# Where the low halves of 32 input-projection weight tiles are made: VectorE's subtraction, or ScalarE and an accumulating transfer

## The chip, the core and the metric

One Trainium2 chip, one of its cores. The metric is device time in microseconds (us) of one execution, the median of several runs. All times are in us unless marked ns. PE is the matrix engine (TensorE), DVE is VectorE, ACT is ScalarE, POOL is GpSimd, SP is SyncE, which only issues transfers here.

## What is computed

One layer of an encoder over 512 tokens of width 1024, all in float32. The part that matters is the first of its three stages, the token mixer, which begins with one wide projection:

```python
def token_mixer(xn, w_in, b_in, ...):
    proj = xn @ w_in + b_in
    (h_q, h_f_fwd, h_f_bwd, h_i, h_g,
     m_q, m_k, m_v, m_o,
     m_ig_fwd, m_ig_bwd, m_fg_fwd, m_fg_bwd) = split_cols(proj, IN_SPLITS)
...
    x = x + token_mixer(rmsnorm(x, ...), w_in[l], ...)
    x = x + cross_attention(rmsnorm(x, ...), rmsnorm(mem, ...), w_q, w_kv, w_o)
    x = x + squared_relu_mlp(rmsnorm(x, ...), w_up[l], w_down[l])
    return rmsnorm(x, norm_final)
```

Four HGRN2 heads and four mLSTM heads are scanned in both directions from `proj`; their outputs, normalised and gated, go through `w_out`. Cross-attention and a squared-ReLU MLP follow.

## The kernel before

**Three products for one.** A float32 product is made of three PE products on the faster type `float32r`. Each operand is split in a high half, which is its value rounded to `float32r`, and a low half, which is the value minus the high half. `mm3` (lines 226 to 229) issues high times high, high times low, low times high. Where the weights are the stationary operand (kind "d"), the low half of the weights, `wl`, is first read by the third product, line 229; where they are the moving operand (kind "t"), by the second, line 228.

**Weight blocks.** All weights lie in DRAM as blocks of 128 x 1024 numbers (512 KB), in the order in which they are used, `SEQ`. Block 4 is the gate projection; blocks 0 to 3 and 5 to 36 are the input projection `w_in`; then come the cross-attention's keys and values, and so on. One block is 24 matmuls of 512 columns. `load(i)` has SP fetch block i into a staging tile `st` (3 buffers). `split(i)` makes the halves in `wh` and `wl` (3 buffers each): ACT copies `st` to `wh`, rounding it, and DVE subtracts:

```python
def split_out(dst_hi, dst_lo, src):
    sc.activation(dst_hi, src, AF.Copy)
    v.tensor_tensor(out=dst_lo, in0=src, in1=dst_hi.bitcast(F32), op=ALU.subtract)
```

In the trace the first is line 223 (`wh<-st` on ACT), the second line 224 (`wl<-st,wh` on DVE).

**How far ahead.** `weights(key)` splits blocks i, i+1 and i+2 and loads block i+3 before the matmuls of block i. As there are three buffers, the halves of block i+2 can be written when PE has finished block i-1. So each split begins when a block begins on PE and is used two blocks later.

**What else goes on.** Between the matmuls of the projection, `tick()` advances at most two chains of the heads' scans. Each is a generator: some matmuls, then DVE and ACT work for its next step. `gates_chain` transposes on PE (lines 527 and 556) around a scan on DVE (lines 545 and 547). `head_out` takes squares on ACT (line 443), a power on POOL (line 169), a product on DVE (line 445) and a transpose on PE (line 452). The memory tokens are normalised in the same way: squares on ACT (line 712), a power on POOL, a scaling on DVE (line 716), transposes on PE (line 725). Each engine has one queue that runs in order; a scheduler that works from an own model of the engines sets these orders when the kernel is built.

**POOL's transfers.** `add_block` (line 891) is used by the MLP: POOL issues a transfer of a weight block that is added into a tile in SBUF (`accum_op=ALU.add`); the destination is of type float32. The first transfer of such a sum does not add.

Of the kernel before, what the change touches and what calls it, by code (L numbers as in the profile page):

```python
# [13 lines left out]
AF = mybir.ActivationFunctionType  # L14
ALU = mybir.AluOpType
# [30 lines left out]
def _split_order():  # L46
    def d(m, c0, n):
        return [("d", m, 0, c0 + P * i) for i in range(n)]

    def t(m, k0, c0, n=4):  # L50
        return [("t", m, k0 + 2 * i, c0) for i in range(n)]

    seq = t("in", 0, 1536) + [("d", "gate", 0, 0)]
    for g in (0, 512, 1024, 2048):
        seq += d("in", g, 2)
    for g in (0, 512, 1024):
        seq += d("in", g + 256, 2)
    seq += d("in", 2560, 2) + d("in", 3072, 2) + d("in", 2304, 2)
    seq += t("in", 0, 3584) + d("in", 4096, 2) + d("in", 4352, 2)
    seq += d("in", 2816, 2) + d("in", 3328, 2)  # L60
    seq += d("kv", 0, 8) + t("kv", 0, 1024) + t("kv", 0, 1536)
    seq += t("out", 0, 0) + t("out", 0, 512)
    seq += d("xq", 0, 8)
    seq += t("xo", 0, 0) + t("xo", 0, 512)
    for f in range(4):
        for j in range(4):
            seq += d("up", 1024 * f + P * j, 1) + d("up", 1024 * f + P * (j + 4), 1)
        seq += [("t", "down", 8 * f + 2 * g + k, 0) for g in range(2) for k in (0, 4)]
        seq += [("t", "down", 8 * f + 2 * g + 4, 512) for g in range(2)]
    seq += [("t", "down", 8 * f + 2 * g, 512) for f in range(4) for g in range(2)]  # L70
    return seq


SEQ = _split_order()
# [5 lines left out]
def trunk(ctx: ExitStack, tc: tile.TileContext, x, mem, wpk, vec, cst, lmask, rmask, rows, out):  # L80
# [5 lines left out]
    v, sc, gp, pe = nc.vector, nc.scalar, nc.gpsimd, nc.tensor  # L86
# [6 lines left out]
    def T(tag, w, bufs, dt=F32):  # L93
        return (sb if w == 516 else big).tile([P, w], dt, tag=tag, name=nm(tag), bufs=bufs)
# [103 lines left out]
    def load(i):  # L198
        if i >= NSTREAM or i in st_tiles:
            return  # L200
        t = T("st", 1024, 3)
        nc.sync.dma_start(out=t, in_=wpk[i])
        st_tiles[i] = t

    def split(i):
        if i >= NSTREAM or i in hl_tiles:
            return
        load(i)
        s = st_tiles[i]
        hi, lo = T("wh", 1024, 3, F32R), T("wl", 1024, 3, F32R)  # L210
        split_out(hi, lo, s)
        hl_tiles[i] = (hi, lo)

    def weights(key):
        i = SIDX[key]
        with (tc.high_priority() if i > 2 else ExitStack()):
            for n in range(i, i + 3):
                split(n)
            load(i + 3)
        return hl_tiles[i]  # L220
# [4 lines that stand above are left out]
# [64 lines left out]
    for t in range(4):  # L289
        xt = xtile[t]  # L290
        ss = tiny(1)
        sc.activation(junk, xt, AF.Square, accum_out=ss)
        r, _ = rstd_of(ss, 1, D)
        with tc.high_priority():
            for g in range(2):
                xg = xt[:, g * 512:g * 512 + 512]
                v.scalar_tensor_tensor(out=xg, in0=xg, scalar=r, in1=gmix[g], op0=ALU.mult, op1=ALU.mult)
                ps = smb()
                for k in range(4):
                    pe.transpose(ps[:, k * P:k * P + P], xg[:, k * P:k * P + P], ident)  # L300
                p3 = ps[:, :].rearrange("p (k t) -> p k t", t=P)
                split_out(ap(xT[g], t * P, [1024, 4], [1, P]), ap(xT[g], 512 + t * P, [1024, 4], [1, P]), p3)
        if t < 2:
            split(t)
# [417 lines left out]
    for k in range(8):  # L722
# [4 lines left out]
        hi, lo = ms[k]  # L727
# [168 lines left out]
    def job(f, n):  # L896

        if n >= len(JOBS):
            if f < 3:
                split(SIDX["d", "up", 0, 1024 * (f + 1)] + n - len(JOBS))  # L900
            return None
        p, g = JOBS[n]
        if p in PLAIN:
            i = block(f, g, *PLAIN[p])
            split(i)
            return hl_tiles[i]
        if (f, n) not in jobs_hl:
            s_ = sums[f, SUMS[p], g]
            hi, lo = T("wh", 1024, 3, F32R), T("wl", 1024, 3, F32R)
            split_out(hi, lo, s_)  # L910
            jobs_hl[f, n] = (hi, lo)
            if p == "P6":
                add_block(s_, block(f, g, 1, 0))
        return jobs_hl[f, n]
# [208 lines left out]
```

## Time and profile before

| | |
|---|---|
| median of 3 runs | 877.57 (877.56 to 878.74) |
| the profiled execution, its own time | 877.47 |
| its span, first to last instruction | 875.7 |
| outside the span | 1.8 |
| PE busy | 853.6 (97%) |
| DVE busy | 576.2 (66%) |
| ACT busy | 415.5 (47%) |
| POOL busy | 67.4 (8%) |
| transfers issued by SP: share of 16 DMA engines | 26.1% |
| transfers issued by POOL: share of 16 DMA engines | 17.2% |
| loads of staging tiles, issue to landing, median | 3.3 |

The profile is of one execution. Busy time of an engine counts its instructions; matmuls are pipelined, so that a matmul of 0.39 starts every 0.23. A wait is put down to the instruction whose semaphore came last. The time of a transfer runs from its issue to its landing, when the last byte is there and whoever waits is told.

### The profile page before, as it was taken

What the parts mean: (1) busy time and instruction counts of PE and PEld (TensorE: products, weight loads), DVE (VectorE), ACT (ScalarE), POOL (GpSimd) and SP (SyncE); (2) the same over time, 40 slices, a digit from 0 to 9 for tenths busy, and PEclk for the clock granted to TensorE, in tenths of its full rate; (3) what the DMA queues carried; (4) which work ended last, traced back from release to release, by engine and by line L of the source; (5) the groups of instructions that cost most, each with busy time, mean ns of one, the idle gap of its engine ahead of it and who ended that gap; (6) DMA issues with size and microseconds to landing.
All of it is one profiled execution on the core that took longest, in us unless ns stands there. A gap on an engine that the chain in (4) does not pass through costs nothing.

```text
span 875.7 us, 11191 instructions
## 1 busy us (share of the span) xinstructions
PE 853.6 (97%) x4198; PEld 709.3 (81%) x4198; DVE 576.2 (66%) x1006; ACT 415.5 (47%) x758; POOL 67.4 (8%) x114
## 2 busy tenths in 40 slices
PE   7999999999999999999999999999999999999995
PEld 5887888888887886888888887888888888888884
DVE  5557688779536987654655445776667656766675
ACT  5235343353358658534544355553355345435544
POOL 2000000010001000000000200002200310121001
PEclk9999999999999999999999999999999999999998
DMA  7322222311234223352212772238945993598322
GB/s 261 135 98 79 73 73 73 117 63 50 73 99 117 97 98 120 121 169 84 85 51 71 194 190 82 92 116 212 284 143 127 238 279 109 150 284 217 115 55 96
DMA packets 32680, 113.58 MB, mean 130 GB/s; under 512 B 3761, under 2 KB 3889, under 8 KB 32626
## 3 DMA queue, kind: packets, MB, share of 16 engines
q1 hardware_dynamic: 23120, 78.84, 26.1%
q0 software_dynamic: 9216, 33.56, 17.2%
q8 instruction: 33, 0.54, 0.2%
q10 hardware_dynamic: 290, 0.47, 0.1%
q14 instruction: 21, 0.17, 0.1%
HBM read 110.76 MB, written 2.10 MB: 129 GB/s over the span
## 4 chain that ended last, share of the span: by engine, by line
PE 49%; DVE 1%; ACT 0%; POOL 0%; issue 0%; POOLq 0%; ACTq 0%
PE mm L228 10%; PE mm L229 10%; PE mm L227 10%; PE sm L997 5%; PE sm L999 5%; PE sm L998 5%; PE mm L999 1%; PE mm L998 1%; PE mm L997 1%; PE sm L229 1%; PE sm L228 1%; PE sm L227 1%; PE sm L770 0%; PE sm L827 0%; DVE vv L922 0%; ACT t L756 0%
## 5 line engine op out<-in xcount | busy, mean ns | idle before, releaser
L223 ACT ACTIVATE wh<-st 128x1024 fp32r<-128x1024 f32 x133 | 140.9, 1059 | 233.1 <-PE mm L228 115.4
L224 DVE TENSOR_TENSOR wl<-st,wh 128x1024 fp32r<-128x1024 f32 x133 | 162.7, 1223 | 124.3 <-ACT wh L223 120.6
L227 PE MATMUL mm<-xT,wh 128*128 128x512 f32 x552 | 219.7, 399 | 0.0
L228 PE MATMUL mm<-xT,wh 128*128 128x512 f32 x552 | 216.4, 392 | 0.2 <-DVE xT L776 0.2
L229 PE MATMUL mm<-xT,wl 128*128 128x512 f32 x552 | 215.8, 391 | 0.0
L228 PEld LDWEIGHTS mm<-xT,wh 128*128 128x128 f32 x552 | 103.8, 188 | 22.7 <-DVE xT L776 2.0
L229 PEld LDWEIGHTS mm<-xT,wl 128*128 128x128 f32 x552 | 103.6, 188 | 21.7 <-issue 0.2
L227 PEld LDWEIGHTS mm<-xT,wh 128*128 128x128 f32 x552 | 103.8, 188 | 21.4 <-issue 1.2
L891 POOL DMA_DIRECT2D as<-in_wpk x48 | 36.6, 772 | 312.1 <-DVE wl L224 188.1
L955 DVE SCALAR_TENSOR_TENSOR t<-mm,rg 128x512 f32<-128x512 f32 x32 | 22.1, 691 | 55.2 <-PE mm L229 55.0
L229 PE MATMUL mm<-wh,yT 128*128 128x512 f32 x128 | 50.6, 395 | 0.0
L227 PE MATMUL mm<-wh,yT 128*128 128x512 f32 x128 | 50.5, 394 | 0.0
L228 PE MATMUL mm<-wl,yT 128*128 128x512 f32 x128 | 50.0, 391 | 0.0
L999 PE MATMUL sm<-wh,yT 128*128 128x512 f32 x128 | 49.8, 389 | 0.0
L998 PE MATMUL sm<-wl,yT 128*128 128x512 f32 x128 | 49.8, 389 | 0.0
L997 PE MATMUL sm<-wh,yT 128*128 128x512 f32 x128 | 49.8, 389 | 0.0
L223 ACT ACTIVATE wh<-as 128x1024 fp32r<-128x1024 f32 x24 | 25.5, 1062 | 33.3 <-PE sm L999 23.7
L224 DVE TENSOR_TENSOR wl<-as,wh 128x1024 fp32r<-128x1024 f32 x24 | 29.4, 1225 | 13.9 <-ACT wh L223 13.9
L378 PEld LDWEIGHTS sm<-a,t 128*128 128x128 f32 x224 | 30.1, 191 | 2.2 <-ACT t L368 0.4
L930 DVE TENSOR_TENSOR vv<-vv,sm 128x512 f32<-128x512 f32 x48 | 31.0, 680 | 1.2 <-PE sm L999 1.2
L368 ACT ACTIVATE t<-a 128x512 f32<-128x512 f32 x28 | 18.4, 674 | 26.3 <-DVE a L431 23.8
L378 PE MATMUL sm<-a,t 128*128 128x128 f32 x224 | 30.9, 285 | 0.0
(258 smaller groups left out, 1513.5 us busy)
## 6 DMA issues: line engine op xcount, KB each, us to landing
st<-in_wpk SPq DMA_DIRECT2D x133, 512.0 KB, 3.3
as<-in_wpk POOLq DMA_DIRECT2D x48, 512.0 KB, 6.7
gate<-in_wpk POOLq DMA_DIRECT2D x16, 512.0 KB, 7.2
as<-in_x SPq DMA_DIRECT2D x4, 512.0 KB, 6.5
vv<-in_x SPq DMA_DIRECT2D x8, 256.0 KB, 4.3
out<-vv SPq DMA_DIRECT2D x7, 256.0 KB, 2.3
a<-in_mem SPq DMA_DIRECT2D x2, 512.0 KB, 3.9
t<-in_rows SPq DMA_DIRECT2D x2, 256.0 KB, 5.9
```

The lines of the kernel that those rows point to most:

```text
L223: sc.activation(dst_hi, src, AF.Copy)
L224: v.tensor_tensor(out=dst_lo, in0=src, in1=dst_hi.bitcast(F32), op=ALU.subtract)
L227: pe.matmul(ps, lhsT=ah, rhs=bh, start=first, stop=False)
L228: pe.matmul(ps, lhsT=ah, rhs=bl, start=False, stop=False)
L229: pe.matmul(ps, lhsT=al, rhs=bh, start=False, stop=last)
L378: pe.matmul(ps[:, z], lhsT=kc[:, z], rhs=ap(q2, w * P, [2 * L, P // (2 * L)], [512 + L, 2], [1, L]), start=True, stop=True)
L891: gp.dma_start(out=dst, in_=wpk[idx], **kw)
L930: v.tensor_tensor(out=z, in0=z, in1=ps, op=ALU.add if sign > 0 else ALU.subtract)
L955: v.scalar_tensor_tensor(out=y, in0=ps, scalar=0.0, in1=rrow[:, 0:512], op0=ALU.max, op1=ALU.mult)
L997: pe.matmul(ps, lhsT=ah, rhs=bh, start=new, stop=False, **fl)
L998: pe.matmul(ps, lhsT=ah, rhs=bl, start=False, stop=False, **fl)
L999: pe.matmul(ps, lhsT=al, rhs=bh, start=False, stop=end and k == 1, **fl)
```

## The change

For blocks 5 to 36, DVE's subtraction is gone. ACT writes minus the rounded weights into `wl`, POOL issues a transfer that adds the block from DRAM to it, and ACT writes `wh` as before. The low half is then the weights minus their high half, as before.

```diff
         hi, lo = T("wh", 1024, 3, F32R), T("wl", 1024, 3, F32R)
-        split_out(hi, lo, s)
+        if SEQ[i][1] == "in" and i > 4:
+
+            sc.activation(lo, s, AF.Copy, scale=-1.0)
+            gp.dma_start(out=lo, in_=wpk[i], accum_op=ALU.add)
+            sc.activation(hi, s, AF.Copy)
+        else:
+            split_out(hi, lo, s)
         hl_tiles[i] = (hi, lo)
```

Six lines are added, so line numbers of the changed kernel from there on are larger by 6 (229 for 223, 533 for 527); the new ones are 213 (minus), 214 (the transfer) and 215 (`wh`).

On ACT, the split of block 10 (`wh_548` before, `wh_553` now), with the sigmoids of a forget gate and the copy out of the gates' transposes behind it. Before:

```order
L223 ACTIVATE wh_548<-st_484 128x1024
L343 ACTIVATE a_90_531<-mm_486,vc 128x512
L345 ACTIVATE a_91_532<-mm_486,misc 128x512
L529 ACTIVATE a_64_372<-sm_541 64x512
L223 ACTIVATE wh_603<-st_552 128x1024
```

and now:

```order
L215 ACTIVATE wh_553<-st_489 128x1024
L213 ACTIVATE wl_554<-st_489 128x1024
L349 ACTIVATE a_90_536<-mm_491,vc 128x512
L351 ACTIVATE a_91_537<-mm_491,misc 128x512
L535 ACTIVATE a_64_374<-sm_546 64x512
L215 ACTIVATE wh_609<-st_558 128x1024
L213 ACTIVATE wl_610<-st_558 128x1024
```

One copy more stands ahead of the sigmoids. Blocks 7 to 27 and 32 to 36 are split in this order; the other six have `wl` ahead of `wh`.

On PE, in block 8 (`wh_445` before, `wh_448` now), the gates' transposes (line 527 before, 533 now). Before:

```order
L227 MATMUL mm_554<-xT_86,wh_445 128x512
L228 MATMUL mm_554<-xT_86,wh_445 128x512
L527 MATMUL sm_541<-cs,a_92_537 128x128 x4
L229 MATMUL mm_554<-xT_86,wl_446 128x512
L227 MATMUL mm_554<-xT_86,wh_445 128x512
L228 MATMUL mm_554<-xT_86,wh_445 128x512
L229 MATMUL mm_554<-xT_86,wl_446 128x512
```

and now:

```order
L235 MATMUL mm_560<-xT_86,wl_449 128x512
L233 MATMUL mm_560<-xT_86,wh_448 128x512
L234 MATMUL mm_560<-xT_86,wh_448 128x512
L235 MATMUL mm_560<-xT_86,wl_449 128x512
L233 MATMUL mm_560<-xT_86,wh_448 128x512
L533 MATMUL sm_546<-cs,a_92_542 128x128 x4
L234 MATMUL mm_560<-xT_86,wh_448 128x512
```

They stand five matmuls later, and so do the transposes of line 556 that follow in the next block.

On POOL, in order, the last of the new transfers: those of blocks 34 to 36 (`wl_2023`, `wl_2146`, `wl_2223`), around two transfers for the MLP (line 897) and the powers of the memory's norm (`tiny_2085`, `tiny_2098`), now:

```order
L214 DMA wl_2023<-in_wpk 128x1024
L214 DMA wl_2146<-in_wpk 128x1024
L897 DMA gate_4627<-in_wpk 128x1024
L169 TENSOR_TENSOR tiny_2085<-tiny_2083,misc 128x1
L169 TENSOR_TENSOR tiny_2098<-tiny_2096,misc 128x1
L897 DMA gate_4627<-in_wpk 128x1024
L214 DMA wl_2223<-in_wpk 128x1024
L584 MEMSET t_374_2193 128x2
```

Without the three `wl` rows this is POOL's order of before.

## Rows read from the trace of the kernel before

**Rows 1.** The page's busy time of each engine, share of the span, instructions.
```profile
PE 853.6 (97%) x4198; PEld 709.3 (81%) x4198; DVE 576.2 (66%) x1006; ACT 415.5 (47%) x758; POOL 67.4 (8%) x114
```
**Rows 2.** Stretch of the 32 splits: busy PE, PEld, DVE, ACT, POOL; clock, DMA, GB/s.
```profile
32.00:275.00 243.00, 240.46 (x1280) 204.95 (x1278) 170.82 (x298) 105.07 (x186) 7.89 (x18) 1.00 0.27 87
```
**Rows 3.** Who waited for whom, PE: us in total, times, longest.
```profile
PE sm L452 <- DVE t L445: 2.1, 3, 0.8
...
PE sm L556 <- DVE a L545: 1.7, 1, 1.7
```
**Rows 4.** PE's instructions in time with a wait, 32 to 275: start, duration.
```profile
64.52 0.63 PE L527 MATMUL sm<-cs,a 128*128 128x128 f32 x4 [0.17 <-DVE a L524]
...
69.58 0.43 PE L556 MATMUL sm<-cs,a 64*128 64x64 f32 x4 [1.68 <-DVE a L545]
...
185.88 0.63 PE L452 MATMUL sm<-cs,t 128*128 128x128 f32 x4 [0.43 <-DVE t L445]
...
266.28 0.66 PE L725 MATMUL sm<-cs,a 128*128 128x128 f32 x4 [0.26 <-DVE a L716]
```
**Rows 5.** Costliest groups, the copy: busy, mean ns of one, idle before, releaser.
```profile
L223 ACT ACTIVATE wh<-st 128x1024 fp32r<-128x1024 f32 x133 | 140.9, 1059 | 233.1 <-PE mm L228 115.4
```
**Rows 6.** Tile wl, 30 to 274: DVE's subtractions (ns min/median/max), who waited.
```profile
L224 DVE TENSOR_TENSOR wl<-st,wh x32: 1208/1225/1232, 33.5 to 266.1; 128x1024 fp32r<-128x1024 f32 x32
...
who waited for it (us, times):
busy tenths in 40 slices 0699788576583000000000000000000000000000
```
**Rows 7.** ACT in time: splits of blocks 5, 8, 12, 13, and what follows 13.
```profile
32.41 1.06 ACT L223 ACTIVATE wh<-st 128x1024 fp32r<-128x1024 f32 x1 [3.92 <-PE mm L229]
...
49.00 1.06 ACT L223 ACTIVATE wh<-st 128x1024 fp32r<-128x1024 f32 x1 [1.88 <-PE mm L228]
...
75.08 1.06 ACT L223 ACTIVATE wh<-st 128x1024 fp32r<-128x1024 f32 x1 [1.64 <-issue]
...
80.53 1.06 ACT L223 ACTIVATE wh<-st 128x1024 fp32r<-128x1024 f32 x1 [1.80 <-issue]
81.49 0.67 ACT L343 ACTIVATE a<-mm,vc 128x512 f32<-128x512 f32 x1
```
**Rows 8.** PE in time: first reads of wl of blocks 5, 8 and 12.
```profile
43.50 0.39 PE L229 MATMUL mm<-xT,wl 128*128 128x512 f32 x1
...
61.48 0.39 PE L229 MATMUL mm<-xT,wl 128*128 128x512 f32 x1
...
86.40 0.39 PE L229 MATMUL mm<-xT,wl 128*128 128x512 f32 x1
```
**Rows 9.** POOL's transfers, line 891: issue in ns, min/median/max.
```profile
L891 POOL DMA_DIRECT2D as<-in_wpk x48: 543/850/1208, 480.7 to 837.5; - x48
```
**Rows 10.** Landings of adding transfers issued at 589.99, at 671.58, from 504.66 (two).
```profile
DMA to landing us min/median/max: 7.0/7.0/7.0
...
DMA to landing us min/median/max: 5.2/5.2/5.2
...
DMA to landing us min/median/max: 10.8/11.8/12.9
```
**Rows 11.** Two stretches of the MLP, columns as in rows 2.
```profile
560.00:580.00 20.00, 20.00 (x90) 16.57 (x89) 14.95 (x24) 10.93 (x16) 0.00 (x0) 1.00 0.26 82
...
600.00:620.00 20.00, 20.00 (x90) 16.57 (x89) 12.45 (x15) 7.43 (x7) 5.66 (x8) 1.00 1.03 269
```
**Rows 12.** One stretch of the projection, columns as in rows 2.
```profile
200.00:220.00 20.00, 20.00 (x123) 17.41 (x122) 20.00 (x38) 6.12 (x10) 0.00 (x0) 1.00 0.21 67
```
**Rows 13.** The page's transfers of staging tiles: count, KB, us to landing.
```profile
st<-in_wpk SPq DMA_DIRECT2D x133, 512.0 KB, 3.3
```
**Rows 14.** Before the memory's norm, in time: a POOL transfer, ACT's last square.
```profile
262.59 0.74 POOL L891 DMA_DIRECT2D gate<-in_wpk  x1 [9.88 <-DVE tiny L167]
...
263.20 0.19 ACT L712 ACTIVATION_READ_ACCUMULATOR sm<-a 128x1 f32 x1
```

## The prediction, made before the change was run

> **What bounds the kernel.** The page's busy times come first: PE is busy for 97% of the span, DVE for 66%, ACT for 47% [rows 1]. So a change can gain only where PE stands still. The blocks that it touches are 5 to 36, split between 33 and 267 us; in the stretch from 32 to 275 PE is busy for 240.46 of 243.00 [rows 2], and 243.00 - 240.46 = 2.54 is all that could be gained there. The table of waits says what PE waits for: its largest rows name a scan and a product of DVE [rows 3]. In time, four waits lie in the stretch, 0.17, 1.68, 0.43 and 0.26, which sum to the same 2.54 [rows 4]: the gates' transposes, one head's output and the memory's norm. All end on a DVE instruction, none of them line 224. The view of `wl` itself lists nobody under "who waited" for its 32 subtractions [rows 6]. DVE's relief is therefore worth little by itself, and the question is whether the new path of `wl` is quick enough to stay unseen.
>
> **DVE, ACT, POOL: the work.** DVE loses 32 subtractions at 1.225 [rows 6]: 39.2 us of its 170.82 in the stretch [rows 2]. ACT gets 32 copies of the size of `wh<-st`, 1.059 each [rows 5]: 33.9 us onto 105.07, so 139 of 243. I take the copy with scale -1 at the price of the copy. ACT starts its next instruction 0.96 after a split (80.53 to 81.49) [rows 7], so what is queued behind a split comes 0.96 later. POOL issues 32 transfers at 0.85 [rows 9], 27 us onto 7.89. No engine becomes a bound, and none of this is on the path that sets the end, unless through the waits below.
>
> **The path of a low half.** Before, `wl` was there some 2.3 after the split's start (1.06 on ACT, 1.22 on DVE). Now, where `wh` goes first: 0.96 until the second copy starts, 1.06 for it, some 0.1 to hand over (an estimate), 2.1 in all, then POOL's transfer from issue to landing. The trace has adding transfers of 512 KB, into float32 tiles. Where few are in flight they land after 5.2 and 7.0; in the MLP, where POOL issues several at once, two took 10.8 and 12.9 [rows 10]. The projection is like the first kind: one such transfer in each block, beside one staging load, with the DMA engines 27% busy [rows 2]. I take 7.0, the slower of the two, as the staging load will start at the same moment. Then `wl` is there 9.1 after the split.
>
> How long it has: the split of block 5 starts at 32.41 [rows 7] and PE's first read of its `wl` is at 43.50 [rows 8], 11.1 later. For block 12 it is 75.08 to 86.40, 11.3, for block 8 49.00 to 61.48, 12.5. These are the tightest; where the heads' scans stretch the blocks there is more. So 9.1 fits everywhere, with 2.0 to spare: **0**. A landing has to take 11.1 - 2.1 = 9.0 before PE waits at all. With 10.8, `wl` comes after 12.9 and PE would wait 1.8, 1.6 and 0.4 at these three, 3.8; with 12.9, after 15.0: 3.9, 3.7 and 2.5, 10.1.
>
> The cover is the two blocks that a split runs ahead; were it one block, some 5.5, every block would wait.
>
> *A rule that speaks against the change.* POOL's issues in the MLP take 543 to 1208 ns [rows 9], beside DVE at 62 to 75% [rows 11]; in one stretch of the projection DVE was 100% busy [rows 12]. The Trainium skill, SBUF — State Buffer, "SBUF: two separate sides", warns that a transfer issued by GpSimd can be starved, since VectorE's two-port instructions lock GpSimd out of writing descriptors; its example grows from some 620 to 3100 ns. By that (an estimate from the page) 2.5 more on each landing gives 9.5, and PE would wait some 0.5 at block 5 and 0.3 at block 12: +1. By the rows of the MLP it is 0. No row shows the locked case.
>
> **Queues that are passed.** On POOL each new transfer stands ahead of clears and powers, waiting for ACT's copy. The clears there go into tiles that are filled only after the same split, so nobody is kept. The powers matter at the memory's norm: POOL's order puts block 35's transfer before, block 36's after them. ACT's four squares, the last piece ending at 263.20 + 0.19 [rows 14], come 0.96 later, since block 35's second copy is ahead. But POOL was issuing another transfer from 262.59 to 263.33 [rows 14], and PE's transposes now stand one and two matmuls later, 0.23 and 0.46. So of 0.96 little is left: between -0.26 (the wait goes) and +0.96; I take **0**, since the shift in order and DVE's missing subtraction work against the delay.
>
> At the gates, ACT's extra copy is ahead of the sigmoids, and they feed DVE instructions that stand ahead of the copies for PE's transposes. DVE no longer has to subtract there. The transposes stand five matmuls later, 5 x 0.23 = 1.1, so their wait of 0.17 goes. The scan on DVE starts when they are done and copied out, about 1.0 later, and line 556 also stands 1.1 later: its 1.68 stays. Bounds: -1.85 and +0.96; I take **-0.2**, the row's own wait, as both ends of the gap move together.
>
> At 185.88, squares on ACT are behind block 26's split: +0.96, but DVE's next step had its subtraction of 1.22 in the way. Bounds -0.43 and +0.96; I take **+0.2**.
>
> SP's staging loads wait for a free `st`. It becomes free when ACT's second copy ends, 2.0 after the split, against 2.3 before. A load of 3.3 [rows 13] may become slower beside an adding transfer; it has three blocks of time. **0**.
>
> Does PE slow down where more is transferred? From 560 to 580 the DMA engines are 26% busy, from 600 to 620 fully, and PE ran 90 matmuls in both [rows 11]: **0**.
>
> After 275 nothing is changed but a few places in PE's order, where matmuls and a head's instructions change places; the other two waits of this kind (the 2.1 of line 452 less the 0.43 [rows 3, 4]) may grow or shrink by tenths. **0**, bounds -0.5 and +0.5.
>
> **The sum.** -0.2 + 0.2 = 0 on the profiled execution of 877.47 (a span of 875.7 and 1.8 around it), which is 0.1 under the median of 877.57. I forecast **877.6**: no change that can be measured. What a measurement of this kernel tells from no change is about 0.2%, 1.8 us, so 875.8 to 879.4.
>
> **Rivals.**
>
> 1. *The low half comes late* (slower). An adding transfer beside a staging load, started at the same time, into a tile of type `float32r`, which no row shows, lands after more than 9.0. Then PE waits at the blocks that are not stretched by scans. For it: 10.8 and 12.9 do occur [rows 10], and the destination's type is new. Against it: those two had several others in flight, and the projection's DMA engines are 27% busy. Its time: 877.6 + 3.8 = 881.4 with 10.8, and 887.7 with 12.9. It decides from 9.0 on, and costs the 1.8 that can be measured from 10.0 on (1.0 at block 5, 0.8 at block 12). Chance 0.15.
>
> 2. *GpSimd is locked out while VectorE works* (slower by little). If a two-port instruction of DVE holds up POOL's issue by more than the 1.2 that a row shows at most [rows 9], landings grow by that. For it: DVE is 100% busy in a stretch [rows 12]. Against it: DVE at 62 to 75% in the MLP cost POOL at most 1.2. Once for each instruction of DVE, at most 1.2 more: 8.2 from issue to landing, under 9.0, so 877.6 to 878.6. The Trainium skill's rule (SBUF — State Buffer, same section) would give the +1 above. Chance 0.10.
>
> 3. *ACT's queue becomes the late one* (slower). Each place where PE's wait ends on a chain through ACT grows by 0.96 in full. With the three chains of rows 4 that is +2.9: 880.5. For it: ACT runs in order, and the copies have precedence. Against it: at each of the three a subtraction of 1.22 goes from DVE, the next link. Chance 0.08.
>
> 4. *DVE's relief counts* (faster). If the four waits vanish, -2.54: 875.1. For it: all four end on DVE. Against it: the largest is a scan of DVE that starts on an ACT result, and ACT is later there. Chance 0.07.
>
> **How the numbers follow.** The forecast has 0.60. Rivals 1 and 3 are slower by over 0.2%, 0.15 + 0.08 = 0.23, less 0.03 for the part of them under 879.4: 0.20. Rival 4 is faster, and only if nearly all of 2.54 goes: 0.06. Same: 0.74, the forecast with rival 2 and what is left of the others. The range: down to 876.0, which holds all but the end of rival 4; up to 882.0, which takes in rival 3 (880.5) and rival 1 at 10.8 (881.4) with 0.6 for blocks that I have not counted, and leaves out about 0.08 of rival 1.
>
> **What would show it.** Right: the profile of the changed kernel has 32 `wl<-st` copies on ACT near 1.06, 32 adding transfers landing in 5 to 8, no PE wait that names a transfer into `wl`, DVE some 39 us less busy, and PE's waits in the stretch within 1 us of 2.54. Wrong: PE waits at line 235 for `wl`, at blocks 5, 12 and 8 first; landings over 9; POOL issues over 1.2; or the wait of line 556 gone.

## The result, and the profile after

The changed kernel takes 881.59 us in the median of 15 runs, the kernel before 878.45 in runs of the same session: the ratio is 1.0035, with a 95% interval of 1.0029 to 1.0042. So it is slower by some 3.1 us. That lies in the range that was given, but the likeliest case, no change that can be measured, is out. One of the 15 runs took 1746.12 and is left out of the ratio; the others lie in two groups, six from 879.06 to 880.08 (mean granted clock 0.994 to 0.996) and eight from 881.51 to 883.04 (0.992 to 0.994), and the profiled execution, 880.08, is of the first.

The profiled execution of the changed kernel has a span of 878.3, 2.6 more than before. Its busy times, and the stretch of the 32 splits and ten microseconds of it (stretch, length, busy PE, PEld, DVE, ACT, POOL; granted clock, DMA share, GB/s):

```profile
PE 855.2 (97%) x4198; PEld 711.1 (81%) x4198; DVE 543.5 (62%) x974; ACT 445.7 (51%) x790; POOL 96.9 (11%) x146
```
```profile
32.00:275.00 243.00, 239.40 (x1271) 204.43 (x1270) 135.23 (x262) 133.98 (x215) 38.51 (x57) 0.99 0.66 152
70.00:80.00 10.00, 8.35 (x32) 6.78 (x33) 5.35 (x8) 5.86 (x9) 0.95 (x2) 0.83 0.47 110
```

The first line already splits the loss. PE has the same 4198 instructions as before [rows 1] but is busy for 1.6 more (855.2 - 853.6), and idle for 1.0 more (878.3 - 855.2 = 23.1, against 875.7 - 853.6 = 22.1). Longer busy time with equal work points to the clock: the third line has a granted clock of 0.83, where the same ten microseconds of the kernel before read

```profile
70.00:80.00 10.00, 10.00 (x45) 8.29 (x45) 7.43 (x12) 5.72 (x7) 0.00 (x0) 1.00 0.32 103
```

The idle time: PE's table of waits of the changed kernel (us in total, times, longest), and the four waits of the stretch in time (start, duration, in brackets the wait), to be laid beside [rows 3, 4]:

```profile
PE sm L458 <- DVE t L451: 3.3, 4, 1.1
...
PE sm L562 <- DVE a L551: 1.7, 1, 1.7
PE sm L533 <- DVE a L530: 0.9, 1, 0.9
```
```profile
66.59 0.63 PE L533 MATMUL sm<-cs,a 128*128 128x128 f32 x4 [0.87 <-DVE a L530]
71.65 0.43 PE L562 MATMUL sm<-cs,a 64*128 64x64 f32 x4 [1.67 <-DVE a L551]
188.98 0.63 PE L458 MATMUL sm<-cs,t 128*128 128x128 f32 x4 [0.76 <-DVE t L451]
269.27 0.66 PE L731 MATMUL sm<-cs,a 128*128 128x128 f32 x4 [0.23 <-DVE a L722]
```

No row names a transfer into `wl`. What grew is the wait at the gates' first transposes, 0.17 to 0.87, and the one at a head's output, 0.43 to 0.76. The first has its origin in VectorE and GpSimd (their instructions in time, around it):

```profile
63.88 0.57 DVE L353 TENSOR_SCALAR a<-a,misc 128x512 f32<-128x512 f32 x1 [4.41 <-ACT a L349]
64.46 1.83 DVE L354 TENSOR_SCALAR a<-a,misc 128x512 f32<-128x512 f32 x1
66.21 0.23 DVE L530 COPY a<-tiny 128x16 f32<-128x16 f32 x2
```
```profile
63.57 0.97 POOL L214 DMA_DIRECT2D wl<-in_wpk  x1 [5.73 <-ACT wl L213]
64.11 0.96 POOL L528 MEMSET a<- 128x512 f32 x1
64.86 0.68 POOL L541 MEMSET a<- 64x512 f32 x1
65.33 0.68 POOL L542 MEMSET a<- 64x512 f32 x1
```

Line 354, a `tensor_scalar` of 128x512, takes 1.83. All eight of its kind before (as line 348; ns min/median/max) were alike:

```profile
L348 DVE TENSOR_SCALAR a<-a,misc x8: 473/479/482, 63.7 to 139.6; 128x512 f32<-128x512 f32 x8
```

What is new beside it are the three clears for the gates' scan. Before, GpSimd did them with nothing else to do (the first of the three in the line below); now they stand behind the transfers of blocks 5 to 10 in its queue, and the last of these waits for ScalarE until 63.57. So the clears run 44 us later, on top of VectorE.

```profile
19.98 0.53 POOL L522 MEMSET a<- 128x512 f32 x1
```

Behind the two waits, 0.87 and 1.67, eight matmuls of PE stand 0.43 apart instead of 0.23, the lower of its two levels (1.2 GHz for 2.4); the first and the last of them, and the next:

```profile
73.57 0.63 PE L234 MATMUL mm<-xT,wh 128*128 128x512 f32 x1
...
76.56 0.53 PE L235 MATMUL mm<-xT,wl 128*128 128x512 f32 x1
76.92 0.39 PE L233 MATMUL mm<-xT,wh 128*128 128x512 f32 x1
```

8 x 0.20 = 1.6, as much as the whole of the added busy time. Counted matmul by matmul, it is this place that makes the difference: the 201st matmul of 512 columns into `mm` starts at 62.84 before and at 63.06 now, 0.22 later; the 241st at 75.06 and 77.60, 2.54 later; the last at 837.18 and 839.62, 2.44 later. So 2.3 arise at the gates, 0.7 as waits and 1.6 as clock.

The new path itself did what was said of it (the copy on ACT and the issue on POOL in ns, min/median/max; the time from issue to landing in us):

```profile
L213 ACT ACTIVATE wl<-st x32: 1040/1044/1062, 32.4 to 268.3; 128x1024 fp32r<-128x1024 f32 x32
L214 POOL DMA_DIRECT2D wl<-in_wpk x32: 863/876/1187, 33.8 to 272.7; - x32
...
DMA to landing us min/median/max: 6.5/7.8/8.8
```

### The profile page after: what moved, and what is told of

The parts are those of the page before. It is cut to its first block, busy times and chain, and to the rows that moved or that the text cites. A ratio compares the mean times of both kernels' runs of the same rounds, so it can differ in the third digit from the quotient of the medians.

```text
span 878.3 us, 11267 instructions
## 1 busy us (share of the span) xinstructions
PE 855.2 (97%) x4198; PEld 711.1 (81%) x4198; DVE 543.5 (62%) x974; ACT 445.7 (51%) x790; POOL 96.9 (11%) x146
## 4 chain that ended last, share of the span: by engine, by line
PE 49%; DVE 1%; ACT 0%; POOL 0%; issue 0%; POOLq 0%; ACTq 0%
PE mm L234 10%; PE mm L235 10%; PE mm L233 10%; PE sm L1003 5%; PE sm L1004 5%; PE sm L1005 5%; PE mm L1005 1%; PE mm L1004 1%; PE mm L1003 1%; PE sm L235 1%; PE sm L234 1%; PE sm L233 1%; PE sm L776 0%; PE sm L833 0%; DVE vv L928 0%; ACT t L762 0%
## 5 line engine op out<-in xcount | busy, mean ns | idle before, releaser
L230 DVE TENSOR_TENSOR wl<-st,wh 128x1024 fp32r<-128x1024 f32 x101 | 123.6, 1224 | 77.3 <-ACT wh L229 76.5
L961 DVE SCALAR_TENSOR_TENSOR t<-mm,rg 128x512 f32<-128x512 f32 x32 | 22.1, 691 | 55.1 <-PE mm L235 55.0
L214 POOL DMA_DIRECT2D wl<-in_wpk x32 | 29.4, 917 | 188.3 <-ACT wl L213 188.3
L213 ACT ACTIVATE wl<-st 128x1024 fp32r<-128x1024 f32 x32 | 33.5, 1046 | 22.7 <-PE mm L234 22.7
```

Of the source, the lines that this page charges most:

```text
L213: sc.activation(lo, s, AF.Copy, scale=-1.0)
```

## The experiments

Theory A: the clears, put behind the new transfers, collide with VectorE's `tensor_scalar`; PE's wait behind it grows, and the lower clock follows. Theory B: ScalarE's extra copy makes the gates late. Theory C: the transfers' traffic does it. Times are ratios to the kernel before, run beside it on the same chip.

**1. The clears on VectorE.**

```diff
-        gp.memset(lp[:, 0:512], 0.0)
+        v.memset(lp[:, 0:512], 0.0)
...
-        gp.memset(Fr[0:64, 0:512], 0.0)
-        gp.memset(mr[0:64, 0:512], 0.0)
+        v.memset(Fr[0:64, 0:512], 0.0)
+        v.memset(mr[0:64, 0:512], 0.0)
```

> The changed kernel, with the three clears for the gates' scan (128x512, and 64x512 twice) on VectorE instead of GpSimd. Theory A (the clears, queued behind the new transfers, run on GpSimd beside VectorE's tensor_scalar of line 354 and stretch it from 0.48 to 1.83 us; the two waits of TensorE that follow, 0.87 and 1.67, are followed by a stretch at the lower clock): line 354 back to 0.48, but VectorE now has some 0.5 of its own for the 128x512 clear ahead of it, so the wait at line 533 falls from 0.87 to 0 to 0.3, the granted clock from 70 to 80 us is 1.00 again, and the time is 1.5 to 2.7 us under the changed kernel's: ratio to before 1.0005 to 1.0018. Theory B (ScalarE's extra copy makes the gates late): the wait stays at 0.8 or more and the ratio at 1.0030 to 1.0040. Theory C (the traffic of the transfers slows TensorE or the gates): the ratio stays at 1.0030 to 1.0040 too, with landings over 8 us or matmuls longer than 0.39 us outside the stretch behind the gates.

Measured: 0.9992 (0.9983 to 1.0000). Its VectorE in time:

```profile
64.39 0.49 DVE L354 TENSOR_SCALAR a<-a,misc 128x512 f32<-128x512 f32 x1
```

The `tensor_scalar` is back at 0.49, PE does not wait at line 533 at all, the wait at line 562 is 1.18, and the clock from 70 to 80 is 1.00. All 32 copies and transfers are still there, so B and C by themselves cannot be the cause of the 3.1. The gain was a little larger than expected, as the second wait shrank too.

**2. The clears early on GpSimd.** The tiles are taken and cleared at the start of the program, so that the clears stand ahead of every transfer.

```diff
     ml = {}
+    ml["lp"], ml["fm"] = A4(), A4()
+    gp.memset(ml["lp"][:, 0:512], 0.0)
+    gp.memset(ml["fm"][0:64, 0:1024], 0.0)
...
-        lp = A4()
-        gp.memset(lp[:, 0:512], 0.0)
+        lp = ml["lp"]
```

> The changed kernel, with the tiles for the gates' scan taken and cleared at the start of the program, so that the clears stand on GpSimd ahead of all 32 transfers; nothing else is moved. Theory A (clears collide with VectorE's tensor_scalar): that tensor_scalar takes 0.48 again, the wait at the first gates' transposes goes from 0.87 to under 0.2, the next one stays at 1.6 to 1.7, the granted clock from 70 to 80 us is 1.00, ratio to before 1.0000 to 1.0010. Theory B (ScalarE's extra copy): wait 0.8 or more, ratio 1.0030 to 1.0040. Theory C (the transfers' traffic): ratio 1.0030 to 1.0040.

Measured: 0.9995 (0.9986 to 1.0004), as theory A has it, a little under its range; `tensor_scalar` 0.49, no first wait, a clock of 1.00. This version is less clean than the first: with the tile free early, the gates' transposes also moved 18 places forward on PE, which the expectation had not foreseen, and their second wait is 1.29.

**3. The collision without the change.** The kernel before, with one GpSimd copy of a single column in each of blocks 5 to 10, so that the clears come as late as in the changed kernel.

```diff
         split_out(hi, lo, s)
+        if 4 < i < 11:
+            gp.tensor_copy(tiny(1), hi[:, 0:1].bitcast(F32))
```

> The kernel before, with one GpSimd copy of a 128x1 column from the high half in each of blocks 5 to 10, so that the clears stand behind them in GpSimd's queue as they do in the changed kernel; there is no transfer into wl, VectorE subtracts and ScalarE copies once. Theory A: the clears run near 62 to 65 us, beside VectorE's work, and stretch what VectorE does there by 1 to 1.4 us; a wait at the first gates' transposes of 0.7 to 1.5 instead of 0.17, and if the lower clock follows such waits, it comes here as well: ratio 1.0015 to 1.0040 without any transfer. If the clears happen to run where VectorE's instruction isn't a tensor_scalar of two ports, the stretch is under 0.3 and the ratio under 1.0010. Theories B and C (extra copy, traffic): nothing here, ratio 0.9995 to 1.0005.

Measured: 1.0032 (1.0019 to 1.0044), without a single transfer into `wl` or copy on ScalarE more. VectorE, GpSimd (the last of the six added copies, then the clears), PE and the clock there:

```profile
63.05 1.32 DVE L349 TENSOR_SCALAR a<-a,misc 128x512 f32<-128x512 f32 x1
64.30 0.82 DVE L350 TENSOR_SCALAR a<-a,misc 128x512 f32<-128x512 f32 x1
```
```profile
61.93 1.24 POOL L213 COPY tiny<-wh 128x1 f32<-128x1 f32 x1 [5.36 <-ACT wh L225]
63.11 0.52 POOL L524 MEMSET a<- 128x512 f32 x1
63.57 0.52 POOL L537 MEMSET a<- 64x512 f32 x1
64.04 0.79 POOL L538 MEMSET a<- 64x512 f32 x1
```
```profile
65.42 0.63 PE L529 MATMUL sm<-cs,a 128*128 128x128 f32 x4 [1.29 <-DVE a L526]
70.48 0.43 PE L558 MATMUL sm<-cs,a 64*128 64x64 f32 x4 [1.67 <-DVE a L547]
```
```profile
70.00:80.00 10.00, 9.52 (x37) 7.78 (x38) 6.33 (x9) 4.62 (x6) 0.00 (x0) 0.83 0.15 53
```

This time the clears fell on both `tensor_scalar`s, 1.32 and 0.82 instead of 0.54 and 0.48: 1.12 lost on VectorE, and PE's wait grew by 1.12 (1.29 - 0.17). The clock fell to 0.83 again, and PE's busy time is 855.2, the very number of the changed kernel. This settles theory A. The added copies show the opposite case: five of the six, of one column each, took 1.17 to 1.24 beside a subtraction of VectorE of 1.23; the one at 49.89, which was done before the subtraction began at 50.30, took 0.18.

**4. ScalarE's extra copy alone.** VectorE's subtraction then writes over what the copy left.

```diff
+        if SEQ[i][1] == "in" and i > 4:
+            sc.activation(lo, s, AF.Copy, scale=-1.0)
         split_out(hi, lo, s)
```

> The kernel before, with ScalarE's copy with scale -1 into wl added to blocks 5 to 36; VectorE's subtraction then writes over it, so the result is the same. There is no transfer into wl and the clears are early. Theory A: no collision; the low half comes 1.06 later, which its run-ahead of two blocks hides; what ScalarE is late with (0.96 at each chain) isn't made up by VectorE here, so PE waits grow by 0 to 1 at the gates and at the memory's norm: ratio 1.0000 to 1.0015. Theory B (the extra copy is the cause): ratio 1.0030 to 1.0040, with the wait at the gates' transposes at 0.8 or more. Theory C: ratio 0.9995 to 1.0005.

Measured: 1.0040 (1.0027 to 1.0053), 3.5 us. Theory B's time, but not by its mechanism: the first wait at the gates is gone and the clock stays at 1.00. The idle time is elsewhere, at the heads and in the memory's chain:

```profile
184.67 0.63 PE L454 MATMUL sm<-cs,t 128*128 128x128 f32 x4 [0.94 <-DVE tiny L167]
186.93 0.63 PE L454 MATMUL sm<-cs,t 128*128 128x128 f32 x4 [0.94 <-ACT wh L225]
...
313.20 0.35 PE L229 MATMUL mm<-a,wh 128*128 128x256 f32 x1 [1.62 <-DVE tiny L640]
```

The copy does cost, then, as long as VectorE keeps its subtraction. Not all of it is the copy's own time: the last extra copy starts at 267.1, so the 1.62 at 313.20 has another cause, likely the orders of the engines, which the scheduler sets anew for each kernel. None of the three waits is in the changed kernel, which asks for the opposite run.

**5. VectorE's relief alone.** Blocks 5 to 36 use the high half as low half; the low halves of these weights are left out of the product.

```diff
-        hi, lo = T("wh", 1024, 3, F32R), T("wl", 1024, 3, F32R)
+        hi = T("wh", 1024, 3, F32R)
+        lo = hi if SEQ[i][1] == "in" and i > 4 else T("wl", 1024, 3, F32R)
...
-        split_out(hi, lo, s)
+        if lo is hi:
+            sc.activation(hi, s, AF.Copy)
+        else:
+            split_out(hi, lo, s)
```

> The kernel before, with VectorE's subtraction left out for blocks 5 to 36 and the high half used as the low half there, so the low halves of these weights are left out of the product; ScalarE copies once, there are no transfers into wl, TensorE has as many matmuls. It measures VectorE's relief alone. Theory A with the compensation that the extra copy's run suggests (copy alone 1.0040; copy, transfers and relief with early clears 0.9995): the relief alone is worth 1 to 3 us, from the waits at line 450's transposes (2.1 + 0.6 + 0.43 counted among them) and the gates; ratio 0.9970 to 0.9990. If the relief is worth nothing by itself, as the prediction's forecast had it: 0.9995 to 1.0005, and the extra copy's loss comes from something else.

Measured: 0.9955 (0.9943 to 0.9967), 3.9 us faster, more than was expected (1 to 3). Its waits over 0.3 behind the splits' start are three:

```profile
67.96 0.43 PE L560 MATMUL sm<-cs,a 64*128 64x64 f32 x4 [0.35 <-DVE a L549]
...
319.65 0.52 PE L456 MATMUL sm<-cs,t 128*128 128x128 f32 x3 [0.57 <-ACT t L447]
...
367.43 0.63 PE L456 MATMUL sm<-cs,t 128*128 128x128 f32 x4 [0.98 <-DVE t L449]
```

So the relief (-3.9) and the copy (+3.5), each known to about 1.1 either way, are both large, and together come to -0.4. Neither arises in the stretch of the splits alone: counted by the same matmuls in the profiled executions, about -2.4 and +2.0 arise from the gates to 275, -1.2 and +1.5 behind it. That the two nearly cancel is what the versions with harmless clears show as well: 0.9992 and 0.9995.

**6. The second wait, moved.** One more yield in the gates' chain of the changed kernel, clears left late.

```diff
         yield
+        yield
         v.tensor_tensor(out=Fr[0:64, 0:512], in0=Fr[0:64, 0:512], in1=mr[0:64, 0:512], op=ALU.subtract)
```

> The changed kernel with its late clears, and one more yield in the gates' chain between the scans and the transposes that follow them, which puts these transposes five matmuls (1.1 us) later on TensorE. The collision stays: line 354 near 1.8 us, the wait at line 533 0.8 to 0.9. The second wait, 1.67, shrinks to 0.3 to 0.7. Theory A1 (the lower clock follows the two waits together): the granted clock from 70 to 80 us is 1.00, the time falls by about 1.1 for the wait and 1.7 for the clock against the changed kernel, ratio to before 0.9995 to 1.0010. Theory A2 (the clock falls after the first wait, or for a reason that has nothing to do with the second): the clock stays near 0.83, only the wait's 1.1 goes, ratio 1.0018 to 1.0028.

Measured: 1.0018 (1.0008 to 1.0028), by a way that neither half had foreseen:

```profile
66.07 0.63 PE L533 MATMUL sm<-cs,a 128*128 128x128 f32 x4 [0.87 <-DVE a L530]
72.46 0.43 PE L563 MATMUL sm<-cs,a 64*128 64x64 f32 x4 [1.88 <-DVE a L551]
```
```profile
70.00:80.00 10.00, 8.12 (x38) 6.41 (x37) 6.15 (x8) 6.63 (x9) 1.75 (x2) 1.00 0.55 128
```

The second wait did not shrink, since the scan now waited 1.23 for a late transfer of `rmask`. Yet the clock stayed at 1.00, and PE's busy time is 853.3. So it does not tell the two waits apart; what it shows is the price of the waits without the clock: 23.8 idle against 22.1, 1.7, about what the ratio says (1.6). It also shows that two waits of this size need not bring the lower clock.

**7 and 8. Later transposes, with the clears early.** The same yield in the version of run 2; and, in the other run, besides it one more yield ahead of the transposes in every head's output.

```diff
                         in1=r.unsqueeze(2).to_broadcast([P, 4, P]), op=ALU.mult)
         yield
+        yield
```

> The changed kernel with the early clears, and one more yield between the gates' scans and the transposes that follow, which puts these 14 matmuls later on TensorE. The wait of 1.29 left there goes, nothing else changes: 1.0 to 1.3 us under the version with early clears alone, ratio to before 0.9975 to 0.9985. If what is held up behind the transposes (the high and low half of ar, the exponentials) is needed sooner, the gain is given back at the memory heads, and the ratio stays at 0.9990 to 1.0000.

> As the run before it, with one more yield in every head's output between the scaling by the norm and the transposes, so that these stand later on TensorE. The four waits there, 0.76, 1.10, 0.54 and 0.87, go or shrink to a third: 2 to 3.3 us more, ratio 0.9940 to 0.9965. Where a head's output is the last thing that a stage waits for (at the end of a drain), the added step costs instead: then some of the gain is given back, and the ratio is 0.9965 to 0.9985.

Measured: 0.9979 (0.9969 to 0.9988) for the first, as expected: no wait at the gates is left. The second gave 0.9986 (0.9978 to 0.9995), not 0.9965 or less: the four waits at the heads (3.3 in all) came back as five, some behind other releasers (1.11 behind line 646, 1.03 behind line 451; 3.9 in all), PE's idle time fell by 0.3 only, and its busy time rose by 2.1, the cause of which stays open.

**9. The same yield in the kernel before.**

> The kernel before, with the one more yield between the gates' scans and the transposes that follow. It tells how much of the 0.9979 of the changed kernel with early clears and this yield belongs to the yield alone. The wait of 1.68 goes, the rest stays: ratio 0.9978 to 0.9986 if the yield is all, and the change with early clears is then worth 0 to 0.5 us; 0.9990 to 1.0000 if the transposes' place only helps where VectorE is relieved.

Measured: 0.9978 (0.9969 to 0.9987). The yield is all of the gain of run 7. Both versions beat the kernel before by 0.2% and the changed one by over 0.5%, and the one without the change needs no transfer for it.

**10. Clears beside the scans.**

```diff
+            if dr == 0:
+                for _ in range(4):
+                    gp.memset(lrow[0:4, 0:512], 0.0)
```

> The changed kernel with early clears, and four useless GpSimd clears (4x512, of rows that nobody reads any more) that wait for the first two of the four scans of VectorE, so that they run beside the last two. It asks which of VectorE's instructions the clears hold up. If any instruction of VectorE is held up by GpSimd's port, the third and fourth scan grow from 1.2 by up to the clears' 1.5 to 2 together, the wait at the next transposes from 1.29 to 2.8 or more, ratio to before 1.0010 to 1.0030. If only tensor_scalar and its like (128x512 in 0.48, faster than an element a cycle) are, the scans stay at 1.19 to 1.21 and the ratio at 0.9990 to 1.0000.

Measured: 0.9991 (0.9982 to 1.0000). GpSimd cleared for 2.23 beside the last two scans, which took what they take alone:

```profile
67.22 2.23 POOL L556 MEMSET a<- 4x512 f32 x4 [2.87 <-DVE a L552]
```
```profile
67.14 1.21 DVE L550 TENSOR_TENSOR_SCAN a<-a 4x512 f32<-4x512 f32 x1
68.28 1.19 DVE L552 TENSOR_TENSOR_SCAN a<-a,a 4x512 f32<-4x512 f32 x1
```

**11 and 12. The cover of two blocks.** First the splits were asked for one block ahead, then the high and low halves got two buffers instead of three.

```diff
-            for n in range(i, i + 3):
+            for n in range(i, i + (2 if 5 < i < 35 else 3)):
```

> The changed kernel with early clears, and splits that run one block ahead of the product instead of two for the blocks from 6 to 35. It measures the path of a low half by itself. By the prediction's steps (2.1 on ScalarE, then 7.0 to 7.8 from issue to landing: 9.1 to 9.9; a block of 24 matmuls is 5.5 of TensorE) some 29 blocks then wait 9.1 to 9.9 less 5.5, 3.6 to 4.4 each where no head's work lies between, less where it does: TensorE's waits name the transfer into wl, and the time grows by 50 to 125 us. If the path is in fact shorter than a block, nothing changes; if it is near the 11.1 at which the prediction's rival 1 begins, it grows by 100 to 160.

Measured: 0.9996 (0.9986 to 1.0007). The edit did not do what it was meant to: the splits still start when PE frees the oldest buffer (31.83, 37.27, 42.71), two blocks ahead. It says nothing on the path.

```diff
-        hi, lo = T("wh", 1024, 3, F32R), T("wl", 1024, 3, F32R)
+        hi, lo = T("wh", 1024, 2, F32R), T("wl", 1024, 2, F32R)
```

> The changed kernel with early clears, and two buffers instead of three for the high and low halves (in the MLP, which shares them, too), since the run before left the splits where they were: a split there starts when the oldest buffer comes free. Now a split runs one block ahead. By the prediction's steps, with the landing that the changed kernel shows, a low half is there 2.1 + 7.6 = 9.7 after its split, and a block of 24 matmuls takes 5.5: TensorE waits 4.2 for the transfer into wl at each of the 8 blocks before the heads begin (34 us) and 0 to 2 at the 24 others, where a block lasts 8.2 on average: the time grows by 34 to 80 us in the projection, and waits name wl at lines 234 and 235 (238 to 240 in this kernel's count at most). If the landing is hidden in another way, the projection grows by less than 10. What the MLP loses is read apart, from its own lines.

Measured: 1.0502 (1.0369 to 1.0635), 44 us.

```profile
PE mm L235 <- DMA wl<-in_wpk: 22.6, 16, 4.4
...
PE mm L234 <- DMA wl<-in_wpk: 1.0, 1, 1.0
```
```profile
64.48 0.50 PE L235 MATMUL mm<-xT,wl 128*128 128x512 f32 x1 [4.39 <-DMA wl<-in_wpk]
```

With the same landings (6.4 to 8.5) PE waits for `wl`, 4.4 at most where 4.2 was worked out, 23.6 in all at 17 places, not at every block. Over run 2 the span grew by 41.2: 29.3 of idle time and 11.9 of busy time. Six of the 41.2 arise in the MLP, which shares the buffers. The lower clock comes once more, but it is only a part of the added busy time: near 48, 66 and 84 us some 19 matmuls stand about 0.43 apart, as these do,

```profile
67.24 0.63 PE L233 MATMUL mm<-xT,wh 128*128 128x512 f32 x1
67.67 0.63 PE L234 MATMUL mm<-xT,wh 128*128 128x512 f32 x1
68.10 0.52 PE L235 MATMUL mm<-xT,wl 128*128 128x512 f32 x1
```

which makes about 4 (19 x 0.20, an estimate). Much of the rest is counted at the waits themselves: the matmul ahead of a wait counts with its full 0.39, and the one behind it keeps the next one 0.33 away (64.48 to 64.81), where 0.23 is usual. The expectation's 34 us were to be waits alone.

## Why the prediction was right and wrong

**The path of a low half: right, by little.** Landings were 7.8 in the median, 0.8 over the 7.0 that was taken; the longest, 8.8, is 0.2 under the 9.0 at which PE was to wait. No wait names `wl`, and run 12 shows that the cover of two blocks is what hides it, though with one block not "every block would wait", as the prediction has it: 17 waits were found. The sign "landing in 5 to 8" was missed at its upper end. Rival 1 did not come, with less to spare than its chance of 0.15 suggests.

**The work moved: right.** VectorE's group of subtractions went from 162.7 to 123.6 (39.1; forecast 39.2). The copies cost 1.04 to 1.06 as taken. By the page VectorE's busy time fell by less than the sign of 39 asks for, from 576.2 to 543.5, 32.7.

**"The clears there go into tiles that are filled only after the same split, so nobody is kept": this is the step that failed.** It looked only at who waits for a cleared tile. It did not ask when the clears would then run, and beside what. They had to wait for block 10's copies on ScalarE, ended up beside the `tensor_scalar` whose successor feeds PE, and stretched it by 1.35 (1.83 - 0.48). VectorE's last copy ahead of the transposes came 2.08 later than before (64.13 to 66.21): besides the 1.35 the first `tensor_scalar` started 0.60 later, behind ScalarE's second copy. PE's transposes did stand five matmuls later, as forecast, and PE reached them 1.37 later (64.35 to 65.72), so that 0.70 was left for the wait; "their wait of 0.17 goes" turned into 0.87. Without the stretch it would have gone, as runs 1 and 2 show. The 1.68 at the next transposes stayed, as forecast (1.67). In the term's own numbers: the gates were put at -0.2 and came to +0.7 in waits. The trace of before had the clears at 19.98, an order of POOL's queue that the change turns round; both were there to be read.

**The rule that was weighed, in the wrong direction.** The prediction took the page SBUF — State Buffer of the Trainium skill, "SBUF: two separate sides", for a warning that VectorE holds up GpSimd's descriptors. Issues took 0.88 in the median and 1.19 at most, against 0.85 and 1.21 of before [rows 9], so that did not happen. The same section of the Trainium skill says that the lock works both ways: whichever starts first has the shared ports for the whole instruction, and a two-port instruction of VectorE then waits. The trace agrees with that reading, if this `tensor_scalar` is such an instruction: line 354 ends at 66.29, 0.28 after the last of the three clears by the profile. Which of the two started first the profile does not settle: in run 3 the stretched `tensor_scalar` starts at 63.05, 0.06 ahead of the first clear. The same section of the Trainium skill also says that VectorE's instructions with two SBUF inputs contend only with a GpSimd instruction that reads SBUF; run 10 agrees, as the clears read nothing and the scans kept their 1.21 and 1.19, and so does run 3, whose copies read SBUF and took as long as the subtraction beside them.

**The clock: not in the prediction.** Its sum had waits alone. Of the 2.6 by which the profiled executions differ, 1.6 is the lower clock behind the waits: what was 0.70 at the gates became 2.3 with it.

**"DVE's relief is therefore worth little by itself": wrong, and cancelled by a second error.** Run 5 puts it at -3.9, more than rival 4's 2.54, as waits after 275 shrank too. ScalarE's copy, "none of this is on the path", costs +3.5 by itself (run 4), somewhat more than rival 3's 2.9. The forecast's 0 for the two together was right (-0.4), for a reason that it gave only for single chains: what ScalarE is late with, VectorE no longer has in the way. The runs show that the two prices cancel; that they do so chain by chain is not shown.

**The small terms.** At 188.98 the wait grew by 0.33 (forecast 0.2), at the memory's norm it went from 0.26 to 0.23 (forecast 0), and the waits of line 452 behind 275 grew by 0.2 (forecast 0, bounds 0.5). The waits in the stretch come to 3.53, 0.99 over the 2.54 of before, so that the sign "within 1 us" is only just met. PE's rate beside twice the traffic is unchanged: 100.00 busy from 80 to 180 in both, with 542 and 543 matmuls.

**Luck.** The range reached up to 882.0 for the sake of rivals 1 and 3, and neither came. That 881.59 lies in it is luck: the collision and the clock, which make the loss, were in none of its terms.

What stays open: the ratio says 3.1, the two profiled executions differ by 2.6, and no execution near the median of 881.59 was profiled; and why the clock falls in the changed kernel and in run 3 and not in run 6, with waits of nearly the same size, was not settled.

## What to carry to other kernels

When a change adds something to a queue that runs in order, look not only at who needs the things behind it, but at when they will now run and what the other engines do at that moment: an idle engine's harmless clears can move to the one microsecond where they hurt. Put such clears ahead of the first transfer, or on the engine that would be held up. And a term that moves work from one busy engine to another is the difference of two large prices; measure both ends before calling either of them nothing.

## What the runs showed of the hardware

- Three GpSimd clears stretched a VectorE `tensor_scalar` of 128x512 (float32) from 0.48 to 1.83, and in run 3 two such instructions from 0.54 and 0.48 to 1.32 and 0.82; the clears themselves took 0.96, 0.68 and 0.68 instead of 0.53, 0.52 and 0.52 in the changed kernel. Scans beside four clears were not held up. GpSimd copies of one column took 1.17 to 1.24 beside a VectorE subtraction of 128x1024 (1.23), and 0.18 without one (run 3).
- Eight matmuls at the lower clock cost 1.6 us, twice the added wait ahead of them (0.70). With 23.6 us of waits for transfers (run 12) some 19 matmuls stood that far apart, about 4 us.
- An adding transfer of 512 KB into `float32r` lands 6.5 to 8.8 us after its issue, where such transfers follow one another a block apart (5.4 us and more), each beside one load.
